# A hybrid encoder block: the last two linear attention heads a page or two later among the values' weight pages, the loads of those pages and their operands pinned in program order, and the R stores on ACT's queue

## The chip, the cores and the metric

The kernel runs on one core of a Trainium2 chip. The core has a matrix engine (TensorE, PE in the profile; its weight loads are PEld), a vector engine (VectorE, DVE), a scalar engine (ScalarE, ACT), GpSimd (POOL) and SyncE (SP), which here only issues transfers (DMAs). Each engine works through its own list of instructions in order. The engines wait for each other and for DMAs through semaphores; an engine that issues a DMA first waits for whatever that DMA needs, and everything behind it in that engine's list waits too.

The metric is the device time of one execution in microseconds (us). Shorter is better.

## The reference

One layer of an encoder over 512 frames of 2048 numbers, in float32: a combined projection, banded softmax attention of 16 heads (group A), gated linear attention of 4 heads (group B, "gla" below), an output projection, a gated MLP with a causal convolution, and a per-layer embedding, each after an RMS norm.

```python
h = rms_norm(x, norm_mix_w[i])
proj = h @ w_in[i]
q_a, k_a, v_a, q_g, k_g, v_g, r_g, gate_lr = split_cols(proj, IN_SPLITS)
y_a = chunked_band_attention(q_a, k_a, v_a, att_rel_bias[i])
log_a = (jax.nn.log_sigmoid(gate_lr @ w_gla_gate_up[i] + b_gla_gate[i]) / GLA_GATE_TAU)
o_g = gated_linear_attention(q_g, k_g, v_g, log_a)        # 4 heads, chunks of 64 frames
y_g = rms_norm(o_g, gla_norm_w[i]) * jax.nn.silu(r_g)
x = x + jnp.concatenate([y_a, y_g], axis=-1) @ w_out[i]
...                                                        # gated MLP with convolution, embedding, final norm
```

## The kernel before, in words

**Arithmetic.** Every float32 operand of a large product is split into a high part (written by an ACT copy that rounds, names ending in `_h`) and the rest (a DVE subtraction, `_l`), and three matmuls (high by high, high by low, low by high) stand for one. A weight page is 128 partitions by 1024 columns, 512 KB. `wtile` (line 123) makes one: a load on SP into a raw tile (`_r`), the ACT copy, the DVE subtraction. Raw tiles, high and low parts each come from rings of buffers, so a page cannot be loaded or split before an older page has left its buffer. At the end of `wtile` up to `hold[0]` "chores" are run: loads on SP and accumulating loads on POOL that add pages of weights in DRAM (`va_S`, `wo_S`).

**The stages at the start**, in order of time:
1. The gla values (`vproj`, line 240), two halves c=0 and c=1 of eight weight pages each (`wv`). During c=1, `input_pair` (line 1177) normalizes the input, and `store_pair` (line 290) forms seven operands for the later products, three of which are plain pieces of the input (R11, R21, R22) and four sums and differences (N1, T3, N2, T4). `store_operand` (line 286) writes each piece to DRAM (`h1d`), 8 pairs by 7 pieces of 128 x 256, all on SP's queue.
2. The four gla heads. `gla_proj(hd)` (line 1222) makes a head's gates and its keys and queries: `pk` and `pq`, 48 matmuls each from two weight pages (`wkg`, `wqg`). `gla_core(hd)` (line 1277) is a generator that does the rest of a head in six steps, one for each call of `step(n)`: (1) DVE makes `kd2` and `eb2`; (2) TensorE transposes (`pkt`) and multiplies (`pat`), ACT copies `kT`, DVE masks; (3) `pu`, and the states S on DVE; (4) `po` from states and values, its copies, squares and sums on DVE and ACT, ending in s2h and s2l; (5) the norm: `msw` on TensorE, then `rstd_wide` with two table loads on ACT (logarithm, exponential) and DVE work; (6) DVE scales the head's two halves and SP stores them to DRAM (`ond`, line 1345). Heads 0 and 1 run ahead of the values of group A. Head 2 (`cores[0]`) and head 3 (`cores[1]`) are spread over it: head 2's step 1 stands ahead of `gla_proj(3)`, its step 2 between that head's `pk` and `pq`, its step 3 ahead of the first page.
3. The values of group A (`values_product`, line 1117, called for each product of `PLAIN`), as seven products P1, P2, P6, P5, P7, P3, P4 in place of eight. Each has four weight pages (`wva_P10` to `wva_P13` for P1, and so on: pages 0 to 27 in this order), 12 matmuls a page. An operand of a product, `in_R11` and so on, is loaded back from `h1d` by `Stage.load` (line 350) in two halves, split by `Stage.split` (line 356), and each half serves two pages. At the start of page n the kernel fetches page n+2, then runs what `plan` has for page n: steps of the heads 2 and 3, loads and splits of operands (lines 1386 to 1396), then the 12 matmuls. After each product `values_collect` (line 1139) adds its two banks into a quarter of the values, and when a quarter is done stores it to DRAM (`vad`; the quarters of the upper half on SP, those of the lower on ACT).
4. After that the attention and the products with `w_blk`, the output projection, the MLP and the embedding, from about 317 us to the end.

**What sets the order.** A scheduler places the instructions of each engine. Those that go through the wrappers `vec`, `act` and `ten` while `in_order(True)` holds are kept in program order on their engine; that is so from line 1400 on, and for single steps by `pinned`. Loads on SP are not wrapped: the scheduler places them. POOL's accumulating loads and the SP loads that feed them are kept in program order by a call of their own. Memory of the heads is given back by `gla_done` and taken by the T and R22 operands; the tiles of `h1` (the normalized input in split form, read by `pk` and `pq`) are given back after `gla_proj(3)` and taken by R11, R21, N2 and N1, tile by tile; a small tile `pad`, which POOL clears, lies first in that memory.

Of the kernel before, what the change touches and what calls it, by code (L numbers as in the profile page):

```python
# [8 lines left out]
F32 = mybir.dt.float32  # L9
# [23 lines left out]
PLAIN = ("P1", "P2", "P6", "P5", "P7", "P3", "P4")  # L33
# [9 lines left out]
def encoder_block(ctx: ExitStack, tc: tile.TileContext, A, out):  # L43
    nc = tc.nc
# [25 lines left out]

    vec, act, ten = InOrder(nc.vector), InOrder(nc.scalar), InOrder(nc.tensor)

    def in_order(on):
        for e in (vec, act, ten):
            e.on = on

    ident = cp.tile([P, P], F32, name="ident")
    make_identity(nc, ident)
# [17 lines left out]
    def use_rings(new):  # L96
        rings.update(new)
        for ring in new:
            counts[ring] = 0
# [15 lines left out]
    def psum_mm(name):  # L115
        return pm.tile([P, T], F32, tag="mm", name=name)
# [6 lines left out]
    def wtile(src, name, parts=1, between=None):  # L123
        n = src.shape[1]
        raw = page("wr", name + "_r")
        hi, lo = page("wh", name + "_h", F32R), page("wl", name + "_l", F32R)
        w = n // parts
        for i in range(parts):
            if i and between is not None:
                between()  # L130
            c = slice(i * w, (i + 1) * w)
            nc.sync.dma_start(raw[:, c], src[:, c])
            act.activation(hi[:, c], raw[:, c], AF.Copy)
            vec.tensor_tensor(lo[:, c], raw[:, c], hi[:, c].bitcast(F32), ALU.subtract)
        for _ in range(hold[0]):
            if chores:
                chores.pop(0)()
        return hi, lo
# [146 lines left out]

    def store_operand(xd, op, k, src):
        c = k % 4 * 256
        nc.sync.dma_start(xd[op, k // 4][:, c:c + 256], src)

    def store_pair(xd, k, a, b, t=None):  # L290

# [34 lines left out]
    class Stage:  # L326
# [23 lines left out]
        def load(self, op, g):  # L350
            w = self.n[g] * 256
            t = xtile(op, g, f"{self.name}_{op}{g}")
            self.x[op, g] = t
            nc.sync.dma_start(t[:, 1, :w].bitcast(F32), self.xd[op, g][:, :w])

        def split(self, op, g, body=True, tails=(0, 1)):
            w = self.n[g] * 256
# [346 lines left out]
    for ci, n in enumerate(CHUNKS):  # L704
        for k in range(n // 2):
            for second in range(2):
                f = f0 + k + second * n // 2
# [8 lines left out]
    h1d = operand_scratch("h1", 8)  # L716
# [191 lines left out]
    for a, b in zip(stages[3:], stages[4:]):  # L908
        i0 = base[a.units[-1]]
        for n, p in enumerate(PLAIN):  # L910
            op = PRODUCTS[p][1]
            for g in range(2):
# [4 lines left out]
                k = 3  # L917
                if g and b.chained and op in ("R21", "T4"):
                    at, k = max(at, 15), 0 if op == "R21" else 3
# [6 lines left out]
    for n, p in enumerate(PLAIN):  # L926
        op = PRODUCTS[p][1]
# [4 lines left out]
        at, k = ((8, 1), (8, 1), (9, 1), (12, 1), (11, 3), (12, 3), (13, 3))[n]  # L932
# [150 lines left out]
    def value_page(name, j):  # L1083
        if name[0] == "S":
            return value_sums[name, j]
        return A["w_v_a"][int(name[1]) - 1, 4 * (int(name[2]) - 1) + j]
# [16 lines left out]

    VALUE_SLOTS = {"C11": 3, "C22": 4, "C12": 5, "C21": 7}

    def values_begin():
        v = dict(ps=[psum_mm(f"va{i}") for i in range(4)], pages=[(p, j) for p in PLAIN for j in range(4)], tiles={}, have=set())
        for n in range(2):
            value_fetch(v, n)
        return v  # L1110

    def value_fetch(v, n):
        if n < len(v["pages"]):
            prod, j = v["pages"][n]
            v["tiles"][n] = wtile(value_page(PRODUCTS[prod][0], j), f"wva_{prod}{j}")
# [41 lines left out]
    if True:  # L1157
# [3 lines left out]
        if True:  # L1161
# [8 lines left out]
            for i in range(2):  # L1170
                t = gp.tile([P, T], F32, name=f"attnT{i}")
# [33 lines left out]
            for kt in range(KD):  # L1205
                w = glh[:, kt * 32:kt * 32 + P]
# [15 lines left out]
            def gla_proj(hd, middle=None):  # L1222
                pz = psum_aux("pz")
                nc.tensor.matmul(pz, up2[:, hd * P:(hd + 1) * P], lr, start=True, stop=True)
                b = bgate[:, hd:hd + 1]
                e = gt("e", "e")
                nc.scalar.activation(e, pz, AF.Abs, bias=b)
                nc.scalar.activation(e, e, AF.Exp, scale=-1.0)
                nc.scalar.activation(e, e, AF.Ln, bias=1.0)
                m = gt("lf", "lf")  # L1230
                nc.vector.tensor_scalar(m, pz, b, 0.0, ALU.add, ALU.min)
                nc.vector.tensor_tensor(m, m, e, ALU.subtract)
                cs = gt("cs", "cs")
                nc.vector.tensor_tensor_scan(cs, reset, m, 0.0, ALU.mult, ALU.add)
                cs3 = cs.rearrange("p (c j) -> p c j", j=CHUNK)
                last = cs3[:, :, CHUNK - 1:CHUNK]
                eb = gt("eb", "eb", 2)
                nc.scalar.activation(eb, cs, AF.Exp, scale=1.0 / TAU)
                en = gt("en", "en", 2)
                nc.scalar.activation(en, cs, AF.Exp, scale=-1.0 / TAU)  # L1240
                dd = gt("dd", "dd", 2)
                nc.vector.tensor_tensor(dd.rearrange("p (c j) -> p c j", j=CHUNK), cs3,
                                        last.broadcast_to([P, NCH, CHUNK]), ALU.subtract)
                nc.scalar.activation(dd, dd, AF.Exp, scale=-1.0 / TAU)
                dec = gt("dec", "dec", 2, NCH)
                nc.scalar.activation(dec, last, AF.Exp, scale=1.0 / TAU)
                dec2 = gt("dec2", "dec2", 2, 2 * NCH + TT)
                de = dec.rearrange("p (t c) -> p t c", c=2)
                to_end = dec2[:, 0:NCH].rearrange("p (t c) -> p t c", c=2)
                from_start = dec2[:, NCH:2 * NCH].rearrange("p (t c) -> p t c", c=2)  # L1250
                nc.vector.memset(dec2[:, 0:2 * NCH], 1.0)
                nc.vector.tensor_copy(to_end[:, :, 0:1], de[:, :, 1:2])
                nc.vector.tensor_copy(from_start[:, :, 1:2], de[:, :, 0:1])
                nc.vector.tensor_tensor(dec2[:, 2 * NCH:].rearrange("p (t c) -> p t c", c=1), de[:, :, 0:1], de[:, :, 1:2],
                                        ALU.mult)

                pk = psum_mm("pk")
                proj(pk, [A["w_blk"][20 + hd, i] for i in range(2)], h1, f"wkg{hd}")
                kf = gt("kf", "kf")
                nc.vector.tensor_tensor(kf, pk, rb, ALU.mult)  # L1260
                nc.vector.tensor_tensor(en, kf, en, ALU.mult)
                nc.vector.tensor_tensor(dd, kf, dd, ALU.mult)
                if middle is not None:
                    middle()
                pq = psum_mm("pq")
                proj(pq, [A["w_blk"][16 + hd, i] for i in range(2)], h1, f"wqg{hd}")

                def queries():
                    qf = gt("qf", "kf")
                    vec.scalar_tensor_tensor(qf, pq, float(P) ** -0.5, rb, ALU.mult, ALU.mult)  # L1270
                    vec.tensor_tensor(eb, qf, eb, ALU.mult)

                if middle is None:
                    queries()
                return eb, en, dd, dec2, queries
# [72 lines left out]
            for hd in range(1, 3):  # L1348
                nxt = gla_proj(hd)
# [4 lines left out]
            step = lambda n: next(cores[n], None)  # L1354

            def pinned(f):
                in_order(True)
                f()
                in_order(False)
# [1 line left out]
            pinned(lambda: step(0))  # L1361
            chores.extend(sum_chores(summed[:2]))
            hold[0] = 2
            nxt = gla_proj(3, lambda: pinned(lambda: step(0)))
            hold[0] = 1
            cores.append(gla_core(3, *nxt))
            hctx.close()
# [15 lines left out]
    def at_page(n, *fs):  # L1383
        plan.setdefault(n, []).extend(fs)

    for page_, k in ((1, 0), (3, 0), (4, 0), (2, 1), (4, 1), (5, 1), (6, 1), (8, 1), (9, 1)):
        at_page(page_, lambda k=k: step(k))
    at_page(10, gla_done)
    at_page(16, open_early)
    for op, loads, splits in (("R21", (0, 1), (2, 3)), ("N2", (2, 3), (5, 7)), ("N1", (4, 5), (9, 11)), ("T3", (10, 11), (13, 15)),  # L1390
                              ("R22", (12, 13), (17, 19)), ("T4", (14, 15), (21, 23))):
        for g in range(2):
            at_page(loads[g], lambda op=op, g=g: front.load(op, g))
            at_page(splits[g], lambda op=op, g=g: front.split(op, g))
    at_page(20, lambda: embedding_split(raws["p"], early[0].tile([P, 2, 1024], F32R, tag="ps", name="ps")))
    at_page(25, lambda: free.extend(("r0", "r1", "r3", "r4", "r5", "r2")), issue)

    for g in range(2):
        front.load("R11", g)
    in_order(True)  # L1400
    use_rings({"wr": ("r3", "r4", "r5", "r2", "r0", "r1")})
    va = values_begin()
    for g in range(2):
        front.split("R11", g)
    nxt[-1]()
    step(0)
    for p in PLAIN:
        values_product(va, p)
        if p == "P4":
            prep(0)  # L1410
            prep(1)
        values_collect(va, p)
    pctx.close()
    pp_ = ctx.enter_context(tc.tile_pool(name="banks", bufs=1, space=PSUM, reuse_waits="tile"))
    for t in range(4):
# [11 lines left out]
    for i, (unit, prod) in enumerate(steps[:-4]):  # L1427
# [24 lines left out]
        if i - len(steps) in EARLY:  # L1452
            p, op, g = EARLY[i - len(steps)]
            t = xtile(op, g, "last")
# [234 lines left out]
```

## Time and profile before

| | us |
|---|---|
| median of 3 runs (2271.85 to 2272.82) | 2271.98 |
| the profiled execution | 2271.67 |
| its span on the core | 2269.8 |
| TensorE busy in the span | 2244.2 |
| the values of group A begin on TensorE | 224.6 |
| the values of group A end on TensorE | 317.0 |

The rows that follow are of one profiled execution. In a row of waits: engine, the instruction that waited, by its output and line, what ended the wait; then the sum in us, how often, and the longest. In a row of the timeline: start and length in us, engine, line, operation, output<-inputs, form and count; in brackets the idle time before it and what ended it. SPq is SP issuing a DMA. Line L65 is the wrapper's call, through which every pinned operation goes, so such rows are told apart by their tiles. A time "to landing" counts from the issue of a DMA to the completion that waits can see. The lengths of matmuls overlap, as they are pipelined: what a matmul costs is the distance to the next start, and the chain of waits shows that.

### The profile page before, as it was taken

To read this page: it belongs to the slowest core of one execution; us is meant where nothing else is said; L and a number is where in the kernel's file an instruction comes from. 1 tells how busy PE (TensorE), PEld (TensorE's weight loads), DVE (VectorE), ACT (ScalarE), POOL (GpSimd) and SP (SyncE) were. 2 spreads that over 40 slices of the span, in tenths; PEclk is the share of its full clock that TensorE was granted. 3 is DMA by queue.
4 is the path that set the end of the run, shared out by engine and by line. 5 is a ranking of instruction groups with operands and counts; after the bars stand their busy time and mean duration, and the time that the engine had idled before them with its cause. 6 is when DMAs were issued, how large, how long until landed. Compare 5 with 4: busy or idle time off the path is not lost.

```text
span 2269.8 us, 45122 instructions
## 1 busy us (share of the span) xinstructions
PE 2244.2 (99%) x17960; PEld 2175.6 (96%) x17960; DVE 1878.0 (83%) x2580; ACT 1311.7 (58%) x1925; POOL 182.8 (8%) x225
## 2 busy tenths in 40 slices
PE   9998999999999999999999999999999999999998
PEld 8786889999999999999999999999999999999997
DVE  7555858999788888998888888888898787898987
ACT  6354656777575575555555555555564554666766
POOL 0010001000000001111111100000000100000000
PEclk9998999999999999999999999999999999999999
DMA  7998698877988989999999987777866967869896
GB/s 273 278 274 257 237 300 200 232 212 194 327 300 255 328 250 254 291 286 290 281 277 280 264 233 214 204 220 195 256 245 221 301 219 225 333 237 333 289 288 210
DMA packets 215220, 588.11 MB, mean 259 GB/s; under 512 B 23168, under 2 KB 74624, under 8 KB 215008
## 3 DMA queue, kind: packets, MB, share of 16 engines
q1 hardware_dynamic: 181568, 474.28, 58.1%
q0 software_dynamic: 29952, 107.49, 25.9%
q10 hardware_dynamic: 3488, 3.44, 0.4%
q8 instruction: 141, 2.31, 0.4%
q14 instruction: 71, 0.58, 0.1%
HBM read 506.48 MB, written 141.56 MB: 286 GB/s over the span
## 4 chain that ended last, share of the span: by engine, by line
PE 90%; DVE 4%; DMA 3%; ACT 2%; issue 1%; SPq 0%; DVEq 0%; ACTq 0%
PE accA L65 44%; PE accC L65 22%; PE accB L65 11%; PE va L65 3%; PE pp L65 1%; PE psc L65 1%; PE py L65 1%; DVE wl L65 1%; DMA wv_r<-in_w_v_g 1%; PE ptr L65 1%; DMA l<-in_w_ple_gate 1%; PE v L265 1%; PE v L264 1%; PE v L266 1%; PE po L65 1%
## 5 line engine op out<-in xcount | busy, mean ns | idle before, releaser
L65 DVE TENSOR_TENSOR wl<-s,wh 128x1024 fp32r<-128x1024 f32 (+1 forms) x365 | 438.0, 1200 | 76.0 <-ACT wh L65 75.0
L65 ACT ACTIVATE wh<-l 128x1024 fp32r<-128x1024 f32 (+1 forms) x308 | 319.2, 1037 | 180.8 <-PE accC L65 118.2
L65 DVE TENSOR_TENSOR wl<-l,wh 128x1024 fp32r<-128x1024 f32 (+1 forms) x308 | 367.7, 1194 | 58.6 <-ACT wh L65 58.3
L65 ACT ACTIVATE wh<-s 128x1024 fp32r<-128x1024 f32 (+1 forms) x365 | 378.2, 1036 | 24.0 <-PE accB L65 12.3
L65 ACT ACTIVATE u<-accA 128x256 f32<-128x256 f32 x290 | 109.6, 378 | 371.7 <-PE accA L65 371.5
L65 DVE TENSOR_TENSOR s<-s,l 128x1024 f32<-128x1024 f32 (+1 forms) x168 | 201.5, 1199 | 3.2 <-DMA s<-in_w_blk 3.2
L65 PE MATMUL accA<-up_T,wh 128*128 128x256 f32 x1408 | 178.8, 279 | 0.0
L65 PEld LDWEIGHTS accA<-up_T,wh 128*128 128x128 f32 x1408 | 170.3, 188 | 0.0
L65 DVE SCALAR_TENSOR_TENSOR cv<-u,cw,cv 128x511 f32<-128x511 f32 (+1 forms) x176 | 131.6, 748 | 3.1
L427 POOL DMA_DIRECT2D s<-in_w_up x84 | 74.0, 881 | 738.0 <-DMA s<-in_w_up 306.8
L65 PE MATMUL accA<-up_T,wl 128*128 128x256 f32 x704 | 96.6, 279 | 0.0
L65 DVE TENSOR_TENSOR u<-u,accC 128x256 f32<-128x256 f32 x98 | 41.0, 419 | 60.3 <-PE accC L65 59.1
L65 PE MATMUL accA<-dn_T,wh 128*128 128x256 f32 x704 | 90.4, 279 | 0.0
L65 PE MATMUL accA<-up_R,wh 128*128 128x256 f32 x704 | 89.8, 280 | 0.0
L65 PE MATMUL accB<-up_R,wh 128*128 128x256 f32 x704 | 89.4, 279 | 0.0
L65 PE MATMUL accA<-up_N,wh 128*128 128x256 f32 x704 | 89.4, 279 | 0.0
L65 PE MATMUL accC<-up_N,wh 128*128 128x256 f32 x704 | 89.4, 279 | 0.0
L65 PE MATMUL accC<-up_R,wh 128*128 128x256 f32 x704 | 89.4, 279 | 0.0
L65 ACT ACTIVATE u<-accC 128x256 f32<-128x256 f32 x94 | 35.9, 382 | 90.6 <-PE accC L65 90.0
L65 PEld LDWEIGHTS accA<-up_T,wl 128*128 128x128 f32 x704 | 88.1, 188 | 0.0
L65 PEld LDWEIGHTS accA<-dn_T,wh 128*128 128x128 f32 x704 | 86.1, 188 | 0.0
L65 PEld LDWEIGHTS accA<-up_R,wh 128*128 128x128 f32 x704 | 85.2, 188 | 0.5 <-issue 0.5
(426 smaller groups left out, 5241.5 us busy)
## 6 DMA issues: line engine op xcount, KB each, us to landing
l<-in_w_up SPq DMA_DIRECT2D x132, 512.0 KB, 6.8
s<-in_w_up SPq DMA_DIRECT2D x84, 512.0 KB, 5.9
s<-in_w_up POOLq DMA_DIRECT2D x84, 512.0 KB, 7.4
l<-in_w_dn SPq DMA_DIRECT2D x56, 448.0 KB, 4.8
l<-in_w_blk SPq DMA_DIRECT2D x36, 512.0 KB, 4.8
l<-in_w_out SPq DMA_DIRECT2D x28, 512.0 KB, 5.0
l<-in_w_dn SPq DMA_DIRECT2D x28, 512.0 KB, 5.0
s<-in_w_blk SPq DMA_DIRECT2D x24, 512.0 KB, 4.4
```

The source lines that it names most:

```text
L65: ins = f(*args, **kw)
L264: nc.tensor.matmul(ps[t], h1[kt][:, 0, sl], wh, start=kt == 0, stop=False)
L265: nc.tensor.matmul(ps[t], h1[kt][:, 0, sl], wl, start=False, stop=False)
L266: nc.tensor.matmul(ps[t], h1[kt][:, 1, sl], wh, start=False, stop=kt == KD - 1)
L427: nc.gpsimd.dma_start(t, src("L22" if name == "S1" else "L11"), accum_op=ALU.add)
```

## The change

1. A wrapper `syn` for SP. Loads in `wtile` and in `Stage.load` go through it, and are kept in program order while `in_order(True, True)` holds: from the first page of the values to their end.
2. `store_operand` issues the R pieces of `h1d` on ACT's queue: three of each pair's seven stores, 24 in all.
3. The middle of `gla_proj(3)` is empty. Head 2's step 2 now stands ahead of the first page, and its steps 3 to 6 at pages 1, 2, 4 and 5 (before: step 3 ahead of the first page, 4 to 6 at pages 1, 3 and 4). Head 3's steps 1 to 6 stand at pages 4, 6, 7, 8, 10 and 11 (before: 2, 4, 5, 6, 8 and 9). `gla_done` stands at page 12 in place of 10, `open_early` at 17 in place of 16.
4. The loads of T3 are at page 12 (before 10 and 11), of R22 at 13 and 14 (12 and 13), of T4 at 15 and 16 (14 and 15); the splits of T3 at 14 and 15 (13 and 15).
5. At the start of the values the order is page 0, the two halves of R11 with their splits, page 1 (before: R11's loads, pages 0 and 1, R11's splits).

```diff
+    syn = InOrder(nc.sync)
+
-    def in_order(on):
+    def in_order(on, loads=False):
         for e in (vec, act, ten):
             e.on = on
+        syn.on = loads
...
-            nc.sync.dma_start(raw[:, c], src[:, c])
+            syn.dma_start(raw[:, c], src[:, c])
...
-        nc.sync.dma_start(xd[op, k // 4][:, c:c + 256], src)
+        (nc.scalar if xd is h1d and op[0] == "R" else nc.sync).dma_start(xd[op, k // 4][:, c:c + 256], src)
...
-            nc.sync.dma_start(t[:, 1, :w].bitcast(F32), self.xd[op, g][:, :w])
+            syn.dma_start(t[:, 1, :w].bitcast(F32), self.xd[op, g][:, :w])
...
-            nxt = gla_proj(3, lambda: pinned(lambda: step(0)))
+            nxt = gla_proj(3, lambda: None)
...
-    for page_, k in ((1, 0), (3, 0), (4, 0), (2, 1), (4, 1), (5, 1), (6, 1), (8, 1), (9, 1)):
+    for page_, k in ((1, 0), (2, 0), (4, 0), (5, 0), (4, 1), (6, 1), (7, 1), (8, 1), (10, 1), (11, 1)):
         at_page(page_, lambda k=k: step(k))
-    at_page(10, gla_done)
-    at_page(16, open_early)
-    for op, loads, splits in (("R21", (0, 1), (2, 3)), ("N2", (2, 3), (5, 7)), ("N1", (4, 5), (9, 11)), ("T3", (10, 11), (13, 15)),
-                              ("R22", (12, 13), (17, 19)), ("T4", (14, 15), (21, 23))):
+    at_page(12, gla_done)
+    at_page(17, open_early)
+    for op, loads, splits in (("R21", (0, 1), (2, 3)), ("N2", (2, 3), (5, 7)), ("N1", (4, 5), (9, 11)), ("T3", (12, 12), (14, 15)),
+                              ("R22", (13, 14), (17, 19)), ("T4", (15, 16), (21, 23))):
...
-    for g in range(2):
-        front.load("R11", g)
-    in_order(True)
+    in_order(True, True)
     use_rings({"wr": ("r3", "r4", "r5", "r2", "r0", "r1")})
-    va = values_begin()
+    va = dict(ps=[psum_mm(f"va{i}") for i in range(4)], pages=[(p, j) for p in PLAIN for j in range(4)], tiles={}, have=set())
+    value_fetch(va, 0)
+    for g in range(2):
+        front.load("R11", g)
     for g in range(2):
         front.split("R11", g)
+    value_fetch(va, 1)
     nxt[-1]()
     step(0)
...
         values_collect(va, p)
+    in_order(True)
```

In the built program this stands as follows on SP: head 1's two `ond` stores come ahead of page P10 (before: behind P10, P11, P13 and P21); head 2's two stand between P23 and N1's second half, P60 (before: behind P50); the two `vad` stores of P2's quarter between P61 and P62 (before: behind P53); head 3's two `ond` between P51 and P52 (before: behind P71); the two `vad` stores of P3's quarter between P41 and P42 (before: behind P43).

More of the change, by code (lines that the diff above doesn't have):

```diff
@@ L1104, in encoder_block @@
     VALUE_SLOTS = {"C11": 3, "C22": 4, "C12": 5, "C21": 7}
[L1106 to L1110, printed above, removed]
     def value_fetch(v, n):
@@ L1396, in encoder_block @@
     at_page(25, lambda: free.extend(("r0", "r1", "r3", "r4", "r5", "r2")), issue)
+    in_order(True, True)
+    use_rings({"wr": ("r3", "r4", "r5", "r2", "r0", "r1")})
+    va = dict(ps=[psum_mm(f"va{i}") for i in range(4)], pages=[(p, j) for p in PLAIN for j in range(4)], tiles={}, have=set())
+    value_fetch(va, 0)
     for g in range(2):
         front.load("R11", g)
-    in_order(True)
-    use_rings({"wr": ("r3", "r4", "r5", "r2", "r0", "r1")})
-    va = values_begin()
     for g in range(2):
         front.split("R11", g)
+    value_fetch(va, 1)
     nxt[-1]()
```

## The prediction, before the changed kernel was run

> **What bounds the kernel now.** I read the page's head first, then TensorE's waits, then the stretch of the edit by windows, chain and each engine's timeline.
>
> ```profile
> span 2269.8 us, 45122 instructions
> PE 2244.2 (99%) x17960; PEld 2175.6 (96%) x17960; DVE 1878.0 (83%) x2580; ACT 1311.7 (58%) x1925; POOL 182.8 (8%) x225
> ```
>
> TensorE is busy 99% of the span. Nothing here removes a matmul, so the edit can gain only what TensorE now idles or runs at half clock, and lose whatever new waits it makes. The waits of TensorE that matter here (summed, times, longest), and one each of POOL and of ACT in this part:
>
> ```profile
> PE va L65 <- ACT in_R L65: 5.7, 1, 5.7
> PE pkt L65 <- DVE kd L65: 4.7, 1, 4.7
> PE v L265 <- DVE wv_l L65: 0.8, 1, 0.8
> PE v L264 <- ACT wv_h L65: 0.3, 1, 0.3
> PE pu L65 <- ACT kT L65: 0.3, 1, 0.3
> ...
> POOL pad L1370 <- PE pq L143: 16.1, 1, 16.1
> ...
> ACT wv_h L65 <- DMA wv_r<-in_w_v_g: 23.1, 3, 10.2
> ```
>
> Windows (stretch: length, PE busy, PEld, DVE, ACT, POOL, granted clock, DMA share, GB/s):
>
> ```profile
> 197.34:200.93 3.59, 0.00 (x1) 0.00 (x0) 3.59 (x6) 3.34 (x6) 0.00 (x0) 1.00 0.01 1
> 200.93:207.76 6.83, 5.76 (x25) 5.07 (x26) 6.50 (x12) 1.20 (x2) 0.25 (x2) 0.50 0.65 222
> 217.99:221.40 3.41, 0.96 (x5) 0.50 (x3) 0.00 (x0) 0.00 (x0) 0.00 (x0) 1.00 0.98 259
> 221.41:228.23 6.82, 3.56 (x8) 2.38 (x9) 3.50 (x4) 3.06 (x3) 0.81 (x1) 0.50 1.04 394
> 2255.76:2259.17 3.41, 1.85 (x16) 1.53 (x14) 2.54 (x10) 2.51 (x7) 0.00 (x0) 1.00 0.61 204
> ```
>
> Each of the two large waits is followed by 6.8 us at clock 0.50. The chain around them gives the unit times (start, length, what):
>
> ```profile
> 149.15 0.44 PE pkt L65 x4
> 149.58 1.50 PE pat L65 x16
> ...
> 214.36 0.33 SPq L132
> 214.78 8.71 DMA in_R<-h_R
> ...
> 229.54 3.12 PE po L65 x28
> 232.67 5.60 PE va L65 x24
> ...
> 246.77 1.56 PE pu L65 x6
> ```
>
> A page of the values costs TensorE 2.8 us (5.60 for 24 matmuls, 12 a page). The operand R11 lands only at 223.5, because its load stands on SP behind a weight page that waits for a free buffer.
>
> **What the change removes.** (a) The R stores leave SP, so the late weight page of the gla values (c=1) comes in time: 0.8 + 0.3 = 1.1 us. ACT has to issue 24 stores, about 0.5 us each as SP does (0.98 for the two `ond` below), 12 us; it waited 23.1 us for these pages, which covers them: 0. Were that cover gone, the last wv split would stay as late as it is, and the 1.1 would not be won. (b) `pkt` no longer stands in the middle of pq: 4.7 us, and from 202.0 to 207.76 at half clock, 2.9. (c) R11 second on SP after P10: 5.7, and half clock from 224.6 to 228.2, 1.8. (d) The 0.3 of `pu`, which gets another place. Together 16.5 us.
>
> **What it adds, at the start.** TensorE leaves pk at 197.3. Now it runs on with pq, whose first half has 23 matmuls left, at 5.60 for 24: 202.7, and two more, 203.2. Then it needs the low half of the second weight page, made in the first row below by 204.4: a wait of 1.2. The 22 matmuls left, pkt and pat then end at 211.5.
>
> DVE, ACT and SP rows (start, length; x2 is two instructions):
>
> ```profile
> 203.18 1.22 DVE L65 TENSOR_TENSOR wqg_l<-wqg_r,wqg_h 128x1024 fp32r<-128x1024 f32 x1
> 243.40 0.69 DVE L65 TENSOR_TENSOR nwt<-rg 128x512 f32<-128x512 f32 x1 [1.25 <-ACT rg L65]
> 246.59 1.22 DVE L65 TENSOR_TENSOR wva_P_l<-wva_P_r,wva_P_h 128x1024 fp32r<-128x1024 f32 x1
> 247.73 0.74 DVE L65 SCALAR_TENSOR_TENSOR pair_r<-pair_r,cols,rg 128x512 f32<-128x512 f32 x1
> 248.40 0.74 DVE L65 SCALAR_TENSOR_TENSOR pair_u<-pair_u,cols,rg 128x512 f32<-128x512 f32 x1
> 254.59 0.68 DVE L65 COPY pair_u<-po 128x512 f32<-128x512 f32 x1
> 257.96 0.69 DVE L65 TENSOR_TENSOR s2l<-s,s2h 128x512 fp32r<-128x512 f32 x1 [0.70 <-ACT s2h L65]
> 261.19 1.28 DVE L65 TENSOR_TENSOR pair_r<-pair_r,va 128x512 f32<-128x512 f32 x2
> ```
>
> ```profile
> 239.44 1.28 ACT L65 ACT_TABLE_LOAD   x1
> 242.73 0.63 ACT L65 ACTIVATE rg<-rg 128x512 f32<-128x512 f32 x1
> 244.22 1.06 ACT L65 ACTIVATE pair_r<-va 128x512 f32<-128x512 f32 x2
> 245.17 1.06 ACT L65 ACTIVATE wva_P_h<-wva_P_r 128x1024 fp32r<-128x1024 f32 x1
> 246.12 0.59 ACT L65 ACTIVATE kT<-pkt 128x512 f32<-128x512 f32 x1
> ```
>
> ```profile
> 177.99 0.82 SPq L132 DMA_DIRECT2D wva_P_r<-in_w_v_a  x1
> 181.52 1.49 SPq L132 DMA_DIRECT2D wva_P_r<-in_w_v_a  x2
> ...
> 200.61 0.98 SPq L1345 DMA_DIRECT2D ond<-pair_r  x2
> ```
>
> Before, P10 and three more pages were loaded at 178 to 183, ahead of the stores `ond` of head 1, which hold SP until DVE is done at 200.6. In the order of the changed kernel these stores stand ahead of P10: all first loads start after 201.7. And `pad`, which holds POOL's accumulating loads, waits for the third pq matmul, now at 197.6 instead of 207.0; so two of those run beside the first loads. Median landing in these stretches, and that of the four in_R (min/median/max):
>
> ```profile
> wva_P_r<-va_S SPq DMA_DIRECT2D x10, 512.0 KB, 3.8
> wo_S<-in_w_out POOLq DMA_DIRECT2D x2, 512.0 KB, 7.2
> DMA to landing us min/median/max: 8.7/10.0/11.2
> ```
>
> At 3.8 us nothing is late: 0. At 10.0, R11 (issued near 202.6) lands at 212.6, its splits (1.06 and 1.22) let page 0 begin 3 us late, and P13, whose split stands ahead of the copies of the states that `po` reads on DVE, costs 3 more: 6. I take 3.5, between the two, as one accumulating load of 7.2 us overlaps about half of the first loads.
>
> **What it adds, behind stores on SP.** The loads of pages and operands are now pinned to each other but `ond` and `vad` are not, and the scheduler put them between loads. SP is one queue: what is behind a store waits for the DVE result it stores. I count from T, the end of page 3.
>
> 1. `pkt` of head 3. DVE makes kd after head 2's norm. ACT: two evictions 0.95, a page 0.95, then table to exp as from 239.44 to 243.36, 3.9; DVE 243.40 to 245.46, 2.1; kd 0.7: T+8.8 with hand-overs. TensorE is there at T+6.05 (a 0.45 sum, two pages): wait 2.75.
> 2. `pu` of head 3. Behind kd DVE does another product, P23's low half and head 2's two results (0.6, 1.15, 1.4): T+11.95. Then two `ond`, N11 and P60 are issued, P60 at T+12.9. N11 lands after 3.8, P60 1.3 later (the four in_R, issued over 1.4 us, landed 1.3 apart): T+17.5. ACT's kT stands behind P60's high half: 1.06 + 0.6, T+19.15. TensorE is there at T+8.85 + 1.95 + 2.8 = T+13.6: wait 5.5. Page 7 ends at U = T+23.45.
> 3. `msw` of head 3. P62 stands behind two `vad`, which wait for page 7 and DVE's two sums (1.4): issued U+1.8, landed 5.6, low half done 7.85. Only then DVE copies po; from 254.59 to the end of s2l, 258.65, is 4.05: U+11.9. TensorE (3.1 + 5.6) is there at U+8.7: wait 3.2.
> 4. P52 stands behind head 3's `ond`. ACT three splits, 2.9, then the norm's 3.9 and 2.1, P51 1.15, two results 1.4: U+22.7; P52 issued 23.15, landed 26.95, high 28.0, low 29.2. TensorE is through page 13 at U+24.1, having waited 0.5: wait 3.9, again 0.95 for the low half; P53 and T30, behind it on the same queue, about 1.6 more: 7.0.
> 5. P42 stands behind two `vad` of page 23: high half at +6.7, low +7.9, TensorE there at +5.6: wait 2.1.
>
> The T3 loads, `gla_done` and the pT tile one page or so later cost nothing by themselves: T3 is first read at page 16, four pages or 11 us on; if not covered, that is the 1.6 in 4.
>
> Sum of 1 to 5: 20.55, and from below 0, should the stores be done before the loads behind them are wanted (rival A). In before such stores cost nothing, as loads had run ahead of them: P50 was issued before head 2's.
>
> 6. Clock. The stretch from 2255.76, busy 1.85 of 3.41, was followed by half clock, as was the one from 217.99: a wait of 2 us can bring it. It cost 2.9 and 1.8. After waits 1 and 3 the next wait takes it up; I count it after 2 and 4, 2 each: 4. Ends: 0 and five times 2.9, 14.4.
>
> The Trainium skill (TensorE: Matmul & The Clock Gate, Part 1) has the clock fall only after a whole idle window of about 3.4 us. By that rule only waits 2 and 4 can bring it, and the upper end is 5.8. The stretch with 1.85 us of work contradicts the rule here.
>
> **Sum.** 2271.67 (the profiled execution's own time: span 2269.8 and 1.9 around it; 0.3 under the median of runs, 2271.98) - 16.5 + 1.2 + 3.5 + 20.55 + 4.0 = 2284.4 us.
>
> **Rivals.**
> - A, faster: the stores do not hold the loads up. Place: SP between P23 and P60. It decides if kT is done by T+13.6, for which P60 must be issued at T+7.35 instead of T+12.9; then P62, P52 and P42 would likewise be in time. For it: no `ond` or `vad` held TensorE before. Against: the norm alone runs to T+8.1. Then terms 2 to 6 go: 2271.67 - 16.5 + 1.2 + 3.5 + 2.75 = 2262.6.
> - B, slower still: the accumulating loads take the engines from the first loads, and each wait costs clock. For it: the load issued at 214.36 and the R11 behind it needed 8.7 us. Both upper ends: 2284.4 + 2.5 + 10.4 = 2297.3. The Trainium skill (DMA: Bandwidth & Descriptors, Queues, rings and completion order) says an engine takes queues in turn by packets; by that rule loads beside an accumulation run at half rate, which speaks for B.
> - C, nothing comes of it: the waits are half of what I sum (10.3 instead of 20.55) and the clock holds through them, 2271.67 - 16.5 + 1.2 + 3.5 + 10.3 = 2270.2. For it: each wait is a sum of rows in line, with every hand-over counted. Against: kd, kT and the loads have no other way round.
>
> **Numbers.** What a measurement tells from no change is about 0.2%, 4.5 us: 2267.4 to 2276.5. Forecast 2277 to 2292: 0.56. B, above: 0.20. C: 0.10. A: 0.14. So faster 0.14, same 0.10, slower 0.76. The range 2265 to 2299 leaves out part of A and the end of B.
>
> **What would show it.** In the changed kernel: no wait for in_R of 5.7 and none of `v` for wv_l (removed); PE waits for kT near 5, for msw near 3, and for P52's and P42's halves, and SP's waits for pair_r and pair_u just before late loads; half clock in two to four places between 200 and 320 us; the values ending near 330 instead of 317. Wrong if TensorE goes through pages 6 to 15 without waits.

## The result, and the profile after

The changed kernel takes 2297.99 us (median of 4 runs, 2297.15 to 2299.23), the kernel before 2272.40 (median of 4, 2271.85 to 2274.19): 1.0112 times as long, 95% interval 1.0094 to 1.0129. It is 25.6 us slower. The forecast was slower too, by 12.7 (2284.4); the time lies in the range, at its upper end, near what rival B gave (2297.3).

The head of the profile after (span; busy time of each engine; granted clock of TensorE in 40 slices of 57.4 us):

```profile
span 2296.4 us, 45123 instructions
...
PE 2251.3 (98%) x17960; PEld 2179.0 (95%) x17960; DVE 1878.8 (82%) x2580; ACT 1311.3 (57%) x1925; POOL 182.9 (8%) x225
...
PEclk9999889999999999999999999999999999999999
```

TensorE is busy 7.1 us longer than before with the same 17960 matmuls, which points to the clock, and it is low in the slices from 230 to 344 us. So the loss lies in the values. One window shows it whole: from the first `pkt` (head 0) to the first `pp` matmul, with which the attention begins. Columns: length, then busy time of PE, PEld, DVE, ACT, POOL, clock, DMA share, GB/s. First before, then after:

```profile
148.99:316.82 167.83, 156.89 (x755) 128.39 (x754) 115.46 (x147) 92.56 (x108) 9.14 (x12) 0.96 0.78 252
```

```profile
150.09:345.38 195.29, 167.53 (x755) 135.14 (x754) 116.45 (x147) 91.86 (x108) 9.21 (x12) 0.91 0.67 217
```

The stretch is 27.5 us longer. Length less PE busy is the time that TensorE waited: 10.9 and 27.8. The 755 matmuls are the same, so the difference of the busy times, 10.6, is nearly all clock. In the chain of before a `pq` matmul took 0.43 at clock 0.50 and 0.23 at full clock, so about half of the busy time in a half-clock period is lost; summed over the periods that is 4.7 before and 14.6 after, 9.9 more. What is left, 152.3 and 152.9, is the work at full clock. The waits of TensorE after, in all, times, longest:

```profile
PE va L65 <- ACT wva_P_h L65: 7.2, 2, 4.1
PE pu L65 <- ACT kT L65: 6.2, 1, 6.2
PE po L65 <- DVE S L65: 3.8, 1, 3.8
PE msw L65 <- ACT s2h L65: 3.1, 1, 3.1
PE pkt L65 <- DVE kd L65: 2.7, 1, 2.7
PE plr L1204 <- ACT Vg L273: 2.2, 1, 2.2
...
PE va L65 <- ACT in_R L65: 1.6, 1, 1.6
PE pq L146 <- DVE wqg_l L65: 1.4, 1, 1.4
PE va L65 <- DVE wva_P_l L65: 1.2, 2, 0.8
```

The 5.7 for in_R, the 4.7 for kd in the middle of pq and the 0.8 for `wv_l` of before are gone, and a row of new ones is there: kT and msw, the pages P52 and P42 (the first row, two waits of 3.1 and 4.1, and the last, 0.8 and 0.5), S at the start, and `plr`, which the prediction did not have. (`plr` is a small product for the heads' gates; it stands behind `Vg`, with which ACT copies the gla values out.) Behind kT, msw, P52 and P42 stands the same thing, and behind P10 at the start too, in SP's own list:

```profile
201.71 0.99 SPq L1342 DMA_DIRECT2D ond<-pair_r  x2
202.75 0.46 SPq L65 DMA_DIRECT2D wva_P_r<-in_w_v_a  x1
...
250.38 0.33 SPq L1342 DMA_DIRECT2D ond<-pair_r  x1
251.04 0.33 SPq L1342 DMA_DIRECT2D ond<-pair_u  x1
251.46 0.40 SPq L65 DMA_DIRECT2D in_N<-h_N  x1
251.96 0.86 SPq L65 DMA_DIRECT2D wva_P_r<-va_S  x2
...
266.11 1.07 SPq L1148 DMA_DIRECT2D vad<-pair_r  x2
267.28 1.02 SPq L65 DMA_DIRECT2D wva_P_r<-va_S  x2
...
289.23 0.32 SPq L1342 DMA_DIRECT2D ond<-pair_c  x1
289.66 0.40 SPq L65 DMA_DIRECT2D wva_P_r<-va_S  x1
...
327.90 0.97 SPq L1148 DMA_DIRECT2D vad<-pair_u  x2
328.92 1.92 SPq L65 DMA_DIRECT2D wva_P_r<-in_w_v_a  x2
```

Each store waits for what DVE has yet to write, and the page behind it is issued within 1 us of the store: P10 at 202.75, P60 at 251.96, P62 at 267.28, P52 at 289.66, P42 at 328.92. ACT splits P60 before it makes kT, and TensorE wants kT from 253.2 on; it wants P42 from 332.2 on. The loads then take 7.9, 5.7, 4.8, 3.8 and 6.2 us, in the chain of waits:

```profile
202.75 7.89 DMA wva_P_r<-in_w_v_a
...
251.96 5.71 DMA wva_P_r<-va_S
...
267.28 4.83 DMA wva_P_r<-va_S
...
289.66 3.75 DMA wva_P_r<-va_S
...
328.92 6.15 DMA wva_P_r<-in_w_v_a
```

And behind the long waits the clock falls, with one exception. Six windows of after in pairs, the one with the wait and the one behind it (columns as above). The middle pair, the wait for kd, is the exception: the clock held:

```profile
213.08:216.49 3.41, 1.55 (x6) 0.99 (x7) 1.51 (x2) 2.16 (x3) 0.29 (x1) 1.00 1.03 380
216.49:219.90 3.41, 3.41 (x10) 2.65 (x9) 3.27 (x4) 1.50 (x2) 0.00 (x0) 0.50 1.07 291
243.80:247.21 3.41, 1.55 (x7) 0.93 (x5) 2.09 (x4) 3.25 (x4) 0.00 (x0) 1.00 0.00 0
247.21:250.63 3.42, 2.63 (x22) 2.39 (x23) 3.42 (x6) 0.00 (x0) 0.00 (x0) 1.00 0.00 0
...
254.03:257.44 3.41, 0.00 (x0) 0.00 (x0) 0.00 (x0) 0.00 (x0) 0.00 (x0) 1.00 0.96 333
257.44:264.27 6.83, 4.90 (x12) 3.88 (x13) 5.19 (x7) 3.43 (x4) 0.00 (x0) 0.50 0.05 19
```

### The profile page after: what moved, and what is told of

It reads as the page before. It is cut to its first block, busy times and chain, and to the rows that moved or that the text cites. A ratio compares the mean times of both kernels' runs of the same rounds, so it can differ in the third digit from the quotient of the medians.

```text
span 2296.4 us, 45123 instructions
## 1 busy us (share of the span) xinstructions
PE 2251.3 (98%) x17960; PEld 2179.0 (95%) x17960; DVE 1878.8 (82%) x2580; ACT 1311.3 (57%) x1925; POOL 182.9 (8%) x225
## 4 chain that ended last, share of the span: by engine, by line
PE 88%; DMA 4%; DVE 4%; ACT 2%; issue 1%; SPq 0%; DVEq 0%; ACTq 0%
PE accA L65 43%; PE accC L65 22%; PE accB L65 11%; PE va L65 2%; DMA wva_P_r<-in_w_v_a 1%; DMA on<-ond 1%; PE pp L65 1%; PE psc L65 1%; DVE wl L65 1%; PE ptr L65 1%; PE py L65 1%; PE v L267 1%; DMA wva_P_r<-va_S 1%; PE v L268 1%; PE v L269 1%
```

## The experiments

The theory after the result: (1) the loads pinned in program order, with the stores left free, is what costs; the stores come to stand ahead of loads, and waits and half clock follow. The heads' new pages cost at most the 2.7 of pkt. (2) The start is late by the issue behind head 1's `ond` and by accumulating loads beside the first pages. (3) Half clock is a cost of its own. (4) The R stores on ACT win nothing, since `plr` waits. Rival to (1): the heads at their new pages are late by themselves.

### Fixed loads or moved heads

Three kernels. The first takes the stores out from between the loads:

```diff
-                    nc.sync.dma_start(ond[hd][:, vb], o[vb])
+                    (nc.gpsimd if hd >= 2 else nc.sync).dma_start(ond[hd][:, vb], o[vb])
...
-                (nc.scalar if c else nc.sync).dma_start(vad...
+                (nc.scalar if c else nc.gpsimd).dma_start(vad...
```

> The changed kernel, but the stores ond of heads 2 and 3 and all vad stores are issued by POOL; no store stands between the values' loads on SP any more, the loads keep their fixed order, and the heads their new pages. Theory (late loads behind stores): the waits pu <- kT 6.2, msw <- s2h 3.1, P52's halves 3.9 and P42's 4.6 go, 17.7 in all, and with them the half clock after 257, 278, 295 and 336 us, 10.2; the wait pkt <- kd of 2.7 stays and may bring a drop of its own, 2.5. 2298.0 - 27.9 = 2270.1, to 2273 with that drop. Rival (the heads at their new pages are late by themselves, so other waits on DVE and ACT take the place of these): half or less is won, 2284 or more.

The second lets the loads go free, with the heads where the change puts them:

```diff
-    in_order(True, True)
+    in_order(True)
```

> The changed kernel, but the scheduler places the loads on SP freely, as in the kernel before (it puts P10, P11, P13 and P21 ahead of head 1's ond, head 2's ond behind P51, head 3's behind P73). Theory (late loads behind stores): the waits for kT, s2h, P52 and P42 go with their half clock (27.9), and at the start the waits for in_R and S shrink (3 to 5 with their clock), as the first pages are there early; pkt <- kd 2.7 stays: 2265 to 2270. Rival (the heads' new pages cost): 2284 or more.

The third is the kernel before with the loads pinned and nothing else of the change but the order at the start:

```diff
-    for g in range(2):
-        front.load("R11", g)
-    in_order(True)
+    in_order(True, True)
...
+    value_fetch(va, 0)
+    for g in range(2):
+        front.load("R11", g)
...
+    value_fetch(va, 1)
```

> The kernel before with its own places of the heads and of T3, R22 and T4, and the R stores on SP; only the loads of the values' pages and operands are kept in program order (with page 0, R11, page 1 as in the changed kernel). On SP the stores ond of head 1 then stand ahead of P10, those of head 2 between P22 and N10, those of head 3 between P63 and P50, vad between P61 and P62 and ahead of P42. Theory (the fixed order of the loads, with the stores left free between them, is what costs): waits for late halves appear here too, and the kernel is slower than before by 8 us or more: 2280 to 2300. Rival (the heads' move is what costs): within 3 us of before, 2270 to 2275.

Measured, beside before at 2271.64: stores on POOL 2272.23 (ratio 1.0002, 0.9993 to 1.0011), free loads 2274.17 (1.0011, 1.0001 to 1.0022), before with pinned loads 2301.08 (1.0130, 1.0115 to 1.0145; 1 us above the range expected). Each kernel here has its ratio to its own runs of before, which had medians of 2271.64 to 2272.90, so kernels are best compared by ratio. TensorE's waits with the stores on POOL:

```profile
PE po L65 <- DVE S L65: 4.4, 1, 4.4
PE pkt L65 <- DVE kd L65: 3.0, 1, 3.0
...
PE va L65 <- ACT in_R L65: 1.7, 1, 1.7
```

kT, msw, P52 and P42 are gone, and what stays in the values are the waits of the start and the one for kd. In before with pinned loads they come back at other places, since the stores land between other pages there:

```profile
PE po L65 <- DVE S L65: 10.7, 2, 6.4
PE va L65 <- ACT wva_P_h L65: 10.3, 4, 4.8
PE pkt L65 <- DVE kd L65: 4.6, 1, 4.6
PE va L65 <- DVE wva_P_l L65: 3.6, 4, 1.9
```

So (1) stands and its rival is out: pinning alone makes the kernel before as slow as the changed one, and the changed one without stores between its loads is as fast as before. The forecast for free loads (2265 to 2270) was missed. There R11 again stands on SP behind weight pages, and the first of these could be issued only when one of head 1's `ond` had landed, after 6.4 us of waiting by SP's list. So in_R costs 5.7 as it did before, with 2.9 of half clock (1.8 before):

```profile
PE va L65 <- ACT in_R L65: 5.7, 1, 5.7
```

Moving the heads alone wins nothing.

### The wait for kd

To the free loads, head 3's step 1 one page earlier:

```diff
-    for page_, k in ((1, 0), (2, 0), (4, 0), (5, 0), (4, 1), (6, 1), ...
+    for page_, k in ((1, 0), (2, 0), (3, 1), (4, 0), (5, 0), (6, 1), ...
```

> The run with free loads, and in it head 3's step 1 (kd and eb on DVE) one page earlier, at page 3, ahead of head 2's norm. Theory (pkt waits because DVE makes kd only behind that norm): the wait of 2.7 us before head 3's pkt goes, and nothing takes its place: 2.7 us less than the run with free loads. Rival (the wait is ACT's exponential or another link, and DVE's two products of 1.4 us only push head 2's norm and results back): less than 1 us is won.

2270.68 (0.9993, 0.9983 to 1.0004), against 1.0011 (1.0001 to 1.0022) with free loads. The two intervals overlap a little, so by the times alone the gain is not settled. In the trace the wait for kd (2.7) is gone and no new one came; the one for in_R was 0.6 longer (6.3), and the stretch is 2.0 shorter. So the wait was DVE's order behind head 2's norm, as the prediction's wait 1 had it.

### The start

The stores on POOL as above, without the accumulating loads of wo's second unit:

```diff
     def sum_add(unit, name):
+        if unit.stage.name == "wo" and unit.u == 1:
+            return
```

> The run with the stores of heads 2 and 3 on POOL, without the four accumulating loads of wo's second unit (their sums are left out, so that part of the output projection is computed from wrong weights); three of them run between 199 and 231 us. Theory (the first loads of the values are late for two reasons, their issue behind head 1's ond at 202.8, and the accumulating loads that run beside them): P10 lands 4 to 5 us after its issue instead of 7.9, the waits for in_R (2.2) and S (4.4) shrink to 2 together or less, and the values end 4 to 6 us earlier after head 2's pkt than in that run. Rival (the issue time alone sets it): the waits stay within 1 us, and no time is won.

2264.03 (0.9965, 0.9953 to 0.9978). The two `ond` of head 1 (256 KB) with the accumulating loads beside them, then without, median us to landing last:

```profile
ond<-pair_r SPq DMA_DIRECT2D x2, 256.0 KB, 7.3
```

```profile
ond<-pair_r SPq DMA_DIRECT2D x2, 256.0 KB, 2.2
```

P10 lands 4.0 us after its issue (201.75 to 205.75) where it took 8.0, the waits for in_R and S are gone altogether, and from `pkt` to `pp` the stretch is 160.1 in place of 166.9, a little more than was expected. So (2) holds for the accumulating loads; with them out of the way, no wait of TensorE is left at the start that the late issue behind `ond` could have made.

The other side of the start is R11. In the kernel before, its loads moved to POOL's queue, behind `pad`:

```diff
-        front.load("R11", g)
+        t = xtile("R11", g, f"in_R11{g}")
+        front.x["R11", g] = t
+        nc.gpsimd.dma_start(t[:, 1, :front.n[g] * 256].bitcast(F32), h1d["R11", g][:, :front.n[g] * 256])
```

> The kernel before with one edit: the two loads of R11 are issued by POOL, right behind pad, instead of by SP. The prediction's step (c), 5.7 us of wait and 1.8 of half clock that an earlier R11 would win: 2264 to 2265. Rival (another load or the states S are late next, or R11 is as late beside the accumulating loads): 2268 to 2272.

2265.09 (0.9967, 0.9954 to 0.9979). The loads are issued at 209.5 and 210.9, and the two largest waits left in the stretch are:

```profile
PE pkt L65 <- DVE kd L65: 4.6, 1, 4.6
...
PE pu L65 <- ACT kT L65: 0.3, 1, 0.3
```

### Half clock

The changed kernel with matmuls put where TensorE waits longest; their result is not read, so the output is the same:

```diff
+    def fill(n, m):
+        x, t = front.x[PRODUCTS[PLAIN[n // 4]][1], 0], psum_aux("fill")
+        for _ in range(m):
+            ten.matmul(t, x[:, 0, 0:P], x[:, 0, 0:T], start=True, stop=True)
+
+    for n, m in ((7, 20), (10, 9), (14, 9), (26, 13)):
+        at_page(n, lambda n=n, m=m: fill(n, m))
```

> The changed kernel with 51 more matmuls whose result nobody reads, put on TensorE where it waits longest: 20 ahead of pu (page 7), 9 ahead of msw (page 10), 9 ahead of P52, 13 ahead of P42; at 0.233 us each 4.7, 2.1, 2.1 and 3.0 us, less than the waits there (6.2, 3.1, 3.1, 4.1). The waits themselves stay. Theory (the half clock after these waits is a cost of its own, and comes because TensorE stood idle for 1.9 us or more of 3.41): the half clock after 257, 278, 295 and 336 us goes, 2.45 + 1.71 + 3.04 + 3.02 = 10.2, and the kernel takes 2287 to 2290. Rival (what half clock costs is hidden, as the next operand is not there any sooner): within 2 us of the changed kernel, 2296 or more.

2293.13 (1.0096, 1.0076 to 1.0115). This interval and that of the changed kernel overlap, so by the times alone the gain of 4.9 is not settled. The trace is plainer. The windows of the wait for kT and of the one behind it:

```profile
252.36:255.78 3.42, 3.30 (x15) 2.40 (x13) 0.31 (x1) 1.41 (x2) 0.00 (x0) 1.00 0.61 249
255.78:259.19 3.41, 3.22 (x14) 2.75 (x15) 3.31 (x5) 2.03 (x3) 0.00 (x0) 1.00 0.00 0
```

All four falls of the clock that were aimed at are gone, and so is the one behind S; one at the start stays, and one came behind pkt, of whose wait of 3.5 now 2.35 lie in one window. The two lost 3.4 us, in place of 14.6. From `pkt` to `pp` it takes 188.0 in place of 195.3. So of 11.2 us of half clock 7.3 were won; 2.2 went into waits (17.8, and with the 12.2 of the added matmuls that stand in them 30.0, in place of 27.8) and 1.7 stays unexplained around the added matmuls. The time expected, 2287 to 2290, was missed. In these two traces two thirds of the half clock came back as time, and a fifth was taken up by waits.

### The R stores

The changed kernel with the R stores on SP, and the kernel before with them on ACT:

```diff
-        (nc.scalar if xd is h1d and op[0] == "R" else nc.sync).dma_start(xd[op, k // 4][:, c:c + 256], src)
+        nc.sync.dma_start(xd[op, k // 4][:, c:c + 256], src)
```

> The changed kernel with the R stores back on SP. Theory (on ACT's queue the stores put ACT's evictions of the gla values behind a late page, so plr waits 2.2 us at 98 us, more than the 1.1 that v no longer waits): pkt of head 2 is about 1.1 us earlier than in the changed kernel, no wait of plr, 2296 to 2298. Rival (the stores on ACT help, as the prediction had it): 2299 or more.

> The kernel before with only the R stores moved to ACT's queue. The prediction's step (a): 1.1 us faster, 2270.9. Theory from the profile after (ACT's evictions of Vg come behind a later weight page, plr waits 2.2): 1.1 us slower than before, 2273.1.

2299.85 (1.0123, 1.0108 to 1.0138) and 2273.19 (1.0005, 0.9997 to 1.0014). Neither time can be told from that without the edit. The first missed what was expected (2296 to 2298) and lies where its rival had it; the second is what the theory had, and its interval leaves out the gain of 1.1 that step (a) had (a ratio of 0.9995). The traces do tell the waits. After, ACT and TensorE:

```profile
96.54 1.06 ACT L65 ACTIVATE wkg_h<-wkg_r 128x1024 fp32r<-128x1024 f32 x1 [6.85 <-DMA wkg_r<-in_w_blk]
97.50 0.67 ACT L273 ACTIVATE Vg<-v,rtok 128x512 f32<-128x512 f32 x1
```

```profile
98.22 0.50 PE L1204 MATMUL plr<-h,glh 128*128 128x512 f32 x1 [2.19 <-ACT Vg L273]
```

In the seven traces with the R stores on ACT (the changed kernel included) `plr` waits 1.6 to 2.3 us, and the waits of `v` for `wv` sum to 0 to 1.3; in the five with them on SP `plr` never waits, and `v` waits 1.1 to 2.7. With the R edit the scheduler also loads the second page of `wkg` ahead of the first (landed 93.9 and 96.4 in after); ACT needs the first one first, and `Vg` stands behind it. Whether that swap alone makes the wait was not tried.

### Both together

The changed kernel with free loads, the R stores on SP, head 3's step 1 at page 3, and R11 on POOL (the four edits shown above).

> A version meant to beat both: the changed kernel with the loads placed freely, the R stores on SP, head 3's step 1 at page 3, and the two loads of R11 issued by POOL right behind pad. Theory: against the run with free loads the waits in_R 5.7 with its half clock (3.4) and pkt 2.7 go too: 2264 to 2267, 0.2 to 0.4% faster than before. Rival (R11 on POOL comes beside two accumulating loads and is as late as on SP): 2269 or more.

2259.37 (0.9942, 0.9928 to 0.9956): 12.5 us faster than before, and better than expected.

```profile
149.40:303.63 154.23, 152.19 (x756) 125.04 (x755) 115.43 (x147) 91.59 (x108) 9.88 (x14) 1.00 0.85 275
```

```profile
PE pq L146 <- DVE wqg_l L65: 1.4, 1, 1.4
...
PE va L65 <- DVE wva_P_l L65: 0.5, 1, 0.5
```

In this stretch the clock is full throughout, and TensorE waits 2.0 us. With an empty middle of pq `pad` comes early (198.3), and R11 with it (issued 199.9 and 201.2, landed 205.9 and 208.2), and head 3's `pkt` does not wait. Against before with R11 on POOL the stretch is 5.1 us shorter: that kernel still had the wait of 4.6 for kd and 2.1 of half clock. So here the heads' new order does pay; on top of R11 alone, without the other edits, it was not tried.

All kernels in one table, from the same window and the clock records: length of the stretch, TensorE's waits in it, time lost at half clock, what is left, and from its end to the end of the span.

| kernel | stretch | waits | half clock | left | behind it |
|---|---|---|---|---|---|
| before | 167.8 | 10.9 | 4.7 | 152.3 | 1953.0 |
| after | 195.3 | 27.8 | 14.6 | 152.9 | 1951.0 |
| after, R on SP | 194.3 | 26.3 | 14.7 | 153.3 | 1954.6 |
| before, loads pinned | 196.6 | 29.6 | 13.7 | 153.3 | 1953.9 |
| after, stores on POOL | 166.9 | 11.3 | 3.4 | 152.3 | 1952.2 |
| that, without accumulating loads | 160.1 | 5.1 | 2.8 | 152.2 | 1951.5 |
| after, loads free | 165.7 | 10.1 | 2.9 | 152.7 | 1954.5 |
| that, kd early | 163.7 | 8.4 | 3.2 | 152.1 | 1951.5 |
| after, added matmuls | 188.0 | 17.8 | 3.4 | 166.8 | 1951.8 |
| before, R on ACT | 164.8 | 9.6 | 2.2 | 153.0 | 1953.0 |
| before, R11 on POOL | 159.3 | 5.2 | 2.1 | 152.0 | 1954.4 |
| both together | 154.2 | 2.0 | 0.0 | 152.2 | 1952.6 |

What is left is 152.0 to 153.3 everywhere (with 12.2 more for the added matmuls, and the 1.7 told there), so waits and half clock explain the stretch whole. The last column differs by 3.6 between executions, with no order in it; that after has 2.0 less than before there is no effect of the change.

## Why the prediction was right on the side and wrong in the size

**Removed, 16.5.** (b) and (c) came as worked out: both waits and their half clock are gone, 15.1, and (c) alone, done in the kernel before, won 7.5 in the median's ratio (0.9967) where the step said 5.7 + 1.8. (In its trace the waits shrank by 5.7 and the half clock by 2.6, so that the two figures meet as closely as they do is in part luck.) (d), 0.3, went too. (a), 1.1, failed: the waits of `v` did shrink by about that, but the step asked only whether ACT had time for 24 stores (it had) and not what stands behind ACT's next wait. `plr` waited 2.2 there. The first `pkt` of the changed kernel is 1.1 later than before, not 1.1 earlier. This start differs between executions (149.0 to 152.0 with the R stores on SP, 149.1 to 152.8 on ACT), but the traces explain the spread: without the waits of `v` and `plr` (1.1 to 2.7 on SP, 1.6 to 3.2 on ACT) and the half clock behind them (1.7, in three of the twelve) the start is at 147.5 to 148.2 in all. On average these waits are 1.8 and 2.5, so the R stores on ACT more likely cost something than win it; the runs speak against a gain of 1.1, and how much is lost stays open.

**At the start.** wqg_l 1.2: 1.45 measured. First loads 3.5: 2.15 for in_R and 3.84 for S, 6.0, the upper end. The half weight given to an overlapping accumulating load was too little: P10 took 7.9 in place of 3.8, and 4.0 without them. The Trainium skill (DMA: Bandwidth & Descriptors, Queues, rings and completion order) has each engine serve its queues in turn by packets. 7.9 beside another queue and 4.0 alone agree with that, and rival B had priced it so.

**Behind stores on SP.** Forecast 2.75, 5.5, 3.2, 7.0 and 2.1, 20.55 in all; measured 2.66, 6.21, 3.05, 3.85 and 4.56, 20.33. The mechanism held at every one of the five places, and rival A is out. Within it, P52 was put too high: P53 and T30 behind it came in time. P42 was put too low: a load of the next stage (`l`, issued at 326.2) stands ahead of the `vad` and landed only at 332.5; behind it P42 took 6.15 us from issue to landing in place of 3.8.

**Clock, 4.0: the step that failed.** Measured: 14.6 in six periods, at the upper end that the prediction gave it (14.4; five times 2.9 is 14.5). This 10.6, the 2.2 of (a), 2.5 more at the first loads and 0.6 in small terms, less the 2.0 behind the stretch, make the 13.9 between the forecast 12.7 and the 26.6 between the two spans. That rival B's sum came so near is in part luck: it had the start and the clock at about what they took, but the 2.2 of (a), which it did not have, was offset by the 2.0 behind the stretch, which no edit made. Two things went wrong. The half clock behind the waits of the start (1.7 and 2.7) and behind wait 5 (3.0) was not counted at all. And "the next wait takes it up" was applied as a whole: the added matmuls show that about a fifth is taken up. Only wait 1 cost no clock, as its 2.66 us fell on two windows, 1.86 and 0.80; a window with the same 1.86 idle, the one ahead of 216.49, was followed by half clock, so this was a near thing. The prediction had the row that speaks for the high value, 1.85 us of work in 3.41 and then half clock, and still took 2 for each of two waits.

By the rule of the Trainium skill (TensorE: Matmul & The Clock Gate, Part 1), which wants a whole idle window, only the falls after 254.0 and 332.5 would have come (windows with no work at all, 2.45 and 3.02 lost); the other four came after windows in which TensorE worked 0.4 to 1.6 us. The measurement decides against it here.

**The signs that were named** came: no wait of 5.7 for in_R and none of 0.8 for `wv_l`, waits for kT and msw of 6.2 and 3.1, SP's stores just ahead of the late loads. Half clock came in six places, not two to four, and the values ended at 345, not near 330.

## What to carry to other kernels

Pinning loads to each other on a queue is only safe if what else goes through that queue is pinned or moved too: a store that waits for a late result holds back every load behind it, and moving eight such stores to another queue gave back here all that the pinning had cost. When a wait is priced, price it with its half clock: here it came behind windows of 3.41 us in which TensorE stood idle for 1.9 or more. And when instructions go to another engine, ask not only whether it has the time, but what is queued behind the place where it next waits.

## What was not expected of the hardware

**The clock falls at a share, not at a full window.** The clock's changes lie on a grid of 3.41 us within each trace. In the twelve traces here, over the windows that begin between 80 and 2200 us, 7368 at full clock were followed by full clock, none of which had more than 1.90 us of idle time, and 33 by half clock, of which the least had 1.86; all with 1.92 or more fell. So in this stretch the bound is near 1.9 us idle, 45% busy, and a wait of 2.7 us cost nothing where the grid cut it in 1.86 and 0.80, but 3.05 inside one window cost 1.7. It does not hold everywhere: near the end of the span, where the matmuls in such a window are of 1 and 128 columns, windows with 1.55 to 1.60 us idle were followed by half clock in three of the traces; the row of 2255.76 in the prediction is one. Why they fell earlier was not tried. A half-clock window was followed by full clock when it held 0.43 us of idle time or less, and by another at half clock from 0.66 on (one at 0.38 stayed as well). The periods of the values were 3.41 or 6.83 us long, but for one of 10.24 behind a wait that filled a whole half-clock window.

**Added matmuls keep the clock, and less time is won than half clock is saved.** 51 matmuls that compute nothing of use, put into waits, took 11.2 us of half clock away and shortened the stretch by 7.3, in one trace each; by the medians, 4.9, it is not settled.

**Transfers beside accumulating loads took two to three times as long.** At the start of the values two 256 KB stores took 7.3 us beside them and 2.2 without, the first 512 KB load 8.0 and 4.0. Over the loads of R operands issued between 195 and 240 us, which also queue behind each other, the median was 11.8 and 8.1. The four accumulating loads, where they stood, were worth about 8 us of the whole (1.0002 against 0.9965).
